# Last samples, squares, decay products and mixer sums of a hybrid decoder trunk put at other steps and on other engines

## The chip, the cores and the metric

One core of one Trainium2 chip. The metric is the device time of one execution in microseconds (us); lower is better. A core has a matrix engine (TensorE, PE in the profile, with PEld for its weight loads), VectorE (DVE), ScalarE (ACT), GpSimd (POOL) and SyncE (SP, which here only issues transfers). Each engine works through its own list of instructions in order; POOL and SP also issue DMAs from their lists. Everything is float32; a product is made as three products of rounded parts ("hi" and "lo").

## The reference

One layer of a decoder trunk, for a prompt of 512 positions and for 8 samples of one new position each, together 520 columns (T) in the kernel. Cut to what the change touches:

```
def mixer(xn, conv_prev, gla_prev, w_in, conv_w, gate_w2, gate_b, gla_norm_g, w_out, chunk):
    proj = xn @ w_in
    bg, cg, hin, q, k, v, og, glr = jnp.split(proj, [...], axis=-1)
    cu, conv_new = causal_dwconv(cg * hin, conv_prev, conv_w)      # width 3
    ya = bg * cu
    logf = jax.nn.log_sigmoid((glr @ gate_w2 + gate_b).astype(f32)) / GATE_TAU
    o, s_new = gla_chunked(qh, kh, vh, lf, gla_prev.astype(f32), chunk)
    var = jnp.mean(o * o, axis=-1, keepdims=True)
    o = o * lax.rsqrt(var + EPS) * gla_norm_g...
    yb = o * silu(og)
    out = jnp.concatenate([ya, yb], axis=-1) @ w_out
```

`gla_chunked` is a gated linear attention of 4 heads (keys of 128, values of 256): within a chunk scores with decays, between chunks a state S of 128 x 256 that decays and grows by keys times values, `S = exp(bC) * S + kdec^T v`, with `kdec = k * exp(bC - b)` and queries `q * exp(b)`. After the mixer come an output projection, a gated convolutional feed-forward and a last norm.

## The kernel before, in words

**Order of the work.** The program is one long list written by hand; `InOrder` (L58) ties the engines to the order in which the program issues. In the first stage the input projection goes in *groups*: `group` (L217) makes one 128-column group of outputs, 16 steps of k with six matmuls each (`span`, `mm3`, L140). Weights come in halves of 8 k: loaded by SP (`fetch`, L101), rounded by ScalarE (`high`, L194), the rest taken by VectorE (`low`, L201).

Beside the matmuls other work is fed in at fixed places of a group. After k = 2, 5, 8, 11, 14 (`BEATS`) `beat` (L157) takes one item from `soon`, then one step of the generator at the head of `queue`, then one item from `side`. At the end of a group, and with `group(True)` also after k = 7, `further` (L213) takes one step of the generator in `extra`.

**Heads.** For each head h the groups are k, q, and two of values; for h = 0 only the values, as k and q come before. Then `gla_head(h, ...)` (L938) goes into `queue` and runs, a step per beat, beside the groups of the next head; the last head (h = 3) runs beside the short convolution's groups (`conv_tile`, L870), three for each of two tiles. A head's steps:

- Gate, cumulative sums, then seven levels of scores, `for i, s in enumerate(LEVELS)` (L1094). For a level POOL makes differences (`ptt`, L290), ScalarE the exponential `e` (L988), VectorE two products `L` (L995), PE the scores (L1055, L1070), VectorE puts them through a mask into `at` (L1077).
- Between them the samples, two at a time: `sample_load` (L1017) has SP load the state and v rows broadcast over the partitions; `sample_pair` (L1026) multiplies v by k on ScalarE (L1029), updates the state on VectorE (L1032) and has SP store it; `sample_out` (L1041) multiplies by the queries on PE (L1043). Samples 0, 2, 4 belong to i = 2, 3, 5, samples 6 to the step of the key transposes.
- At i = 4 to 6 the decays `qb` (for queries) and `kc` (for keys) are made: exponentials on ScalarE (L1109, L1115), differences and both products on POOL (L1118, L1120).
- Key step: PE transposes `kc` (L1126), ScalarE copies it to `kt`.
- Four sub-blocks `for c in range(4)` (L1134): PE makes the output from `at` and v (L1138) and, from c = 1 on, from S and `qb` (L1143); ScalarE copies it into `o` (L1147); PE makes the growth of S (L1152), VectorE copies it (L1154) or updates S with it (L1156).
- Then both squares of `o` on ScalarE (L1181, L1182), their sum on POOL (L1183); a beat later PE sums over partitions (L635, in `rsqrt_sums`); ScalarE takes logarithm and exponential (L1189, L1190); a beat later four Newton steps on VectorE (L293 to L296); a beat later VectorE scales `o` (L1195) and it is stored to `o_d`.

**The mixer's sums.** `mixer_sums` (L779) makes sums and differences of quarters of x for a later product with fewer multiplications (a Strassen-like scheme of seven products). It is the generator in `extra` from head 1 on; for each of four g: a load of four tiles by SP; scaling of two tiles on ScalarE (L794); of two more; two sums on VectorE (L704, L698); stores on POOL, two more sums; then stores with the next load. At the very end three `split`s (L121: ScalarE rounds at L123, VectorE takes the rest at L124) in a single step, while POOL stores the last sum.

**The short convolution.** `conv_tile` computes z, and its convolution `conv` is one item of `side`: the last tap on VectorE (`conv_tap`, L608), then the others (`conv_rest`, L615 and, for samples, L618).

**The next stage** (L1790 on) takes over the memory of the heads' pool; its first weight loads (`second_half`, L833) stand on SP behind that. It loads mixer sums (L1753), splits them and runs the seven products (`up_product`, L1397; weights' parts at L1373 and L1377).

Of the kernel before, what the change touches and what calls it, by code (L numbers as in the profile page):

```python
# [12 lines left out]
AF = mybir.ActivationFunctionType  # L13
# [24 lines left out]
def trunk_kernel(  # L38
# [53 lines left out]
    def tmp():  # L92
        return tp.tile([P, T], F32, tag="t", name="t")
# [195 lines left out]
    def ptt(out, a, b, op):  # L289
        nc.gpsimd.tensor_tensor(out, a, b, op=op)  # L290
# [307 lines left out]
    def bank():  # L598
        return msp.tile([P, 512], F32, tag="ms", name="ms")
# [5 lines left out]
    def conv_tap(c, z, w, taps, j, bias=None):  # L605
        tap = w[:, 2 * taps + j : 2 * taps + j + 1]
        if bias is None:
            nc.vector.tensor_scalar(c[:, :T], z[:, 2:], tap, None, op0=ALU.mult)  # L608
        else:
            nc.scalar.activation(c[:, :T], z[:, 2:], AF.Identity, scale=tap, bias=bias)  # L610
# [8 lines left out]
                c[:, NP:T], st[:, i::2], tap(i), c[:, NP:T], op0=ALU.mult, op1=ALU.add  # L619
            )  # L620

    def conv(z, w, taps, j, st):


        c = tmp()
        conv_tap(c, z, w, taps, j)
        conv_rest(c, z, w, taps, j, st)
        return c

    def rsqrt_sums(src):  # L630

        pss = []
# [67 lines left out]
    def add(out, x, y):  # L700
        nc.vector.tensor_tensor(out, x, y, op=ALU.add)  # L701
# [77 lines left out]
    def mixer_sums():  # L779

        def place(n):
            return yt1.tile([P, T + 3], F32, tag=f"y{n}", name="yx")[:, :T]

        for g in (1, 2, 3, 0):
            xg = [place(n) for n in ("l0 h8 l8 h0" if g % 2 else "l1 l4 h4 h0").split()]
            for q, x in enumerate(xg):
                nc.sync.dma_start(two(x), rows_of(xT_d, "mix", g, q))
            yield  # L790
            for q, x in enumerate(xg):
                m = first_tile("mix", g, q // 2)
                for j, h in enumerate(halves(x)):
                    nc.scalar.activation(h, h, AF.Copy, scale=gmix[:, m + j : m + j + 1])  # L794
                if q == 1:
                    yield
            yield
            t1, t3, t4, b22 = xg
            t2 = place("h1")
            sub(t1, t1, t3)  # L800
            minus(t2, t1, b22)
            yield
            if g:
                for f, t in ((5, t1), (4, t2)):
                    nc.gpsimd.dma_start(mt_d[f - 4, g], t)
            sub(t3, b22, t3)
            minus(t4, t2, t4)
            yield
            nc.gpsimd.dma_start(mt_d[3, g], t4)
            if g:  # L810
                nc.gpsimd.dma_start(mt_d[2, g], t3)
        for f, t in ((5, t1), (6, t3), (4, t2)):
            split(t, *form(f, 0))

# [29 lines left out]
    with ExitStack() as mix:  # L846
# [23 lines left out]
        def conv_tile(j):  # L870
            ps = group()
            cgr = tmp()
            evac(ps, cgr[:, :T])
            ps = group()
            hr = tmp()
            evac(ps, hr[:, :T])
            z = next_z()
            nc.vector.tensor_tensor(z[:, 2:], cgr[:, :T], hr[:, :T], op=ALU.mult)
            keep_last(z, j, 8, new_conv_p, new_conv_s)
            c = []  # L880
            side.append(lambda: c.append(conv(z, cw, 8, j, stc[:, j, :])))
            ps = group()
            bgr, ya = tmp(), tmp()[:, :T]
            if j % 2 == 0:
                even[j] = ya = z[:, 2:]
            evac(ps, bgr[:, :T])
            nc.vector.tensor_tensor(ya, bgr[:, :T], c[0][:, :T], op=ALU.mult)
            mixed_done(j, ya)

        in_order = InOrder(nc.gpsimd.engine, nc.sync.engine).after_all()  # L890
        with ExitStack() as gl:
# [46 lines left out]
            def gla_head(h, q, k, vt):  # L938
# [155 lines left out]
                for i, s in enumerate(LEVELS):  # L1094
                    level_scores(Ls.popleft(), s)
                    if i + 2 < len(LEVELS):
                        products()
                    if i + 3 < len(LEVELS):
                        level(LEVELS[i + 3])
                    if i == 5:  # L1100
                        pos = bank()
                        sample_out(0)
                    if i in (2, 3, 5):
                        s0.append(sample_pair({2: 0, 3: 2, 5: 4}[i], *loaded.popleft()))
                    if i in (0, 2, 5):
                        loaded.append(sample_load({0: 2, 2: 4, 5: 6}[i]))
                    if i == 4:
                        qb = gp.tile([P, 4, P], F32, tag="qb", name="qb")
                        nc.scalar.activation(qb, bc, AF.Exp, scale=1.0 / TAU)  # L1109
                        kc = gp.tile([P, 4, P], F32, tag="e", name="kc", bufs=2)  # L1110
                        ptt(
                            kc, bc[:, :, P - 1 : P].to_broadcast([P, 4, P]), bc, ALU.subtract
                        )
                    if i == 5:
                        nc.scalar.activation(kc, kc, AF.Exp, scale=1.0 / TAU)  # L1115
                        ec = gp.tile([P, 4], F32, tag="ec", name="ec")
                        nc.gpsimd.tensor_copy(ec, qb[:, :, P - 1])
                        ptt(qb, qb, q4, ALU.mult)  # L1118
                    if i == 6:
                        ptt(kc, kc, k4, ALU.mult)  # L1120
                    yield

                o = gp.tile([P, 2, T], F32, tag="o", name="o")
# [2 lines left out]
                    nc.tensor.transpose(pb[:, c * P : (c + 1) * P], kc[:, c, :], idn)  # L1126
                kt = gp.tile([P, 4, P], F32, tag="L", name="kt", bufs=2)
                nc.scalar.activation(kt, pb.rearrange("p (c k) -> p c k", c=4), AF.Copy)
                s0.append(sample_pair(6, *loaded.popleft()))
                yield  # L1130


                S = gp.tile([P, DV], F32, tag="S", name="S")
                for c in range(4):  # L1134
                    po = bank()
                    for d in range(2):
                        out = po[:, d * P : (d + 1) * P]
                        nc.tensor.matmul(  # L1138
                            out, vt[:, c, d * P : (d + 1) * P], at[:, c, :],
                            start=True, stop=c == 0,  # L1140
                        )
                        if c:
                            nc.tensor.matmul(  # L1143
                                out, S[:, d * P : (d + 1) * P], qb[:, c, :],
                                start=False, stop=True,
                            )
                    nc.scalar.activation(  # L1147
                        o[:, :, c * P : (c + 1) * P],
                        po[:, :DV].rearrange("p (d i) -> p d i", d=2), AF.Copy,
                    )  # L1150
                    pS = bank()
                    nc.tensor.matmul(pS[:, :DV], kt[:, c, :], vt[:, c, :], start=True, stop=True)  # L1152
                    if c == 0:
                        nc.vector.tensor_copy(S, pS[:, :DV])  # L1154
                    else:
                        nc.vector.scalar_tensor_tensor(  # L1156
                            S, S, ec[:, c : c + 1], pS[:, :DV], op0=ALU.mult, op1=ALU.add
                        )
                    if c == 1:
                        sample_out(4)  # L1160
                        os_ = gp.tile([P, DV], F32, tag="os", name="os")
                        nc.scalar.activation(os_, pos[:, :DV], AF.Copy)
                    if c == 2:
                        pb = bank()
                        for d in range(2):
                            nc.tensor.matmul(
                                pb[:, d * NS : (d + 1) * NS], os_[:, d * P : (d + 1) * P], sel,
                                start=True, stop=True,
                            )
                        nc.scalar.activation(  # L1170
                            o[:, :, NP:T], pb[:, : 2 * NS].rearrange("p (d b) -> p d b", d=2),
                            AF.Copy,
                        )
                    yield
# [2 lines left out]
                store.dma_start(new_gla_p[0, 0, h], S)  # L1177


                sq, sq2, ro = (tmp()[:, :T] for _ in range(3))  # L1180
                nc.scalar.activation(sq, o[:, 0, :], AF.Square)  # L1181
                nc.scalar.activation(sq2, o[:, 1, :], AF.Square)  # L1182
                ptt(sq, sq, sq2, ALU.add)  # L1183
                yield
                for ps, v in zip(rsqrt_sums(sq), halves(sq2)):
                    nc.scalar.activation(
# [50 lines left out]
            for h in range(NH):  # L1237
# [19 lines left out]
                vt = gp.tile([P, 4, DV], F32, tag="vt", name="vt", bufs=2)  # L1257
                v = []
                for d in range(2):
                    ps = group()  # L1260
                    t = gp.tile([P, T], F32, tag="v", name="v", bufs=2)
                    evac(ps, t)
                    v.append(t)
                    soon.append(lambda: None)
                    soon.append(lambda t=t, vt=vt, d=d: v_rows(t, vt, d, 0, 4))
# [842 lines left out]
```

## Time and profile before

| what | value |
|---|---|
| median of 3 runs | 2139.94 us (2136.82 to 2142.19) |
| profiled execution | 2138.38 us |
| its span, first to last instruction | 2136.7 us |
| mean granted TensorE clock | 0.997 |
| instructions | 44234 |
| HBM read, written | 299.65 MB, 80.31 MB |

The profile is of one execution. A row of a timeline gives start and length in us, the engine, the line of the kernel, the operation and the tiles written and read; in square brackets stands how long the engine was idle before it and what ended that. A row of waits names the waiting engine and line, what it waited for, and total, number and longest. The ends of matmuls are modelled. The same source line can serve many callers, so a row is told apart by its tiles and its time.

### The profile page before, as it was taken

The page shows a single profiled execution, that of the slowest core. Times are in us where ns is not written, and L with a number is a line of the kernel's source. Part 1 is how long each engine was busy: PE and PEld are TensorE (multiplying, and loading weights), DVE is VectorE, ACT ScalarE, POOL GpSimd, SP SyncE. Part 2 cuts the span into 40 slices and gives each one's busy share as a digit, 9 for nine tenths or more (in the row PEclk, how much of TensorE's full clock was granted, in tenths as well). Part 3 has the DMA queues.
Part 4 walks back from the last instruction along what each step waited for, and adds up shares of the span by engine and source line. Part 5 has one row for each costly group of instructions (what it writes and reads, how often), then busy time and mean ns, then how long its engine had stood idle before and what let it go on. Part 6 is the DMA issues. An engine that isn't in the chain of part 4 may idle for free.

```text
span 2136.7 us, 44234 instructions
## 1 busy us (share of the span) xinstructions
PE 2109.9 (99%) x17880; PEld 2088.1 (98%) x17880; DVE 1763.6 (83%) x2349; ACT 1121.8 (53%) x1688; POOL 436.0 (20%) x623
## 2 busy tenths in 40 slices
PE   9999999999999999999999999999999999999997
PEld 8999989999999989999999999999999999999997
DVE  6556675988878898988988988988989778888886
ACT  7444543545544686555555555555555554444445
POOL 4212331112234211211311221212212200300000
PEclk9999999999999999999999999999999999999999
DMA  8455646877798996776776676776766875994734
GB/s 257 131 151 171 180 127 183 222 189 205 187 286 240 268 293 157 183 186 175 181 187 172 182 187 169 181 189 167 189 182 183 292 224 150 274 293 131 222 110 159
DMA packets 467757, 417.30 MB, mean 195 GB/s; under 512 B 21769, under 2 KB 426521, under 8 KB 467409
## 3 DMA queue, kind: packets, MB, share of 16 engines
q1 hardware_dynamic: 424209, 289.84, 47.8%
q0 software_dynamic: 43296, 124.57, 22.3%
q8 instruction: 140, 2.29, 0.5%
q14 instruction: 64, 0.52, 0.1%
q10 hardware_dynamic: 48, 0.07, 0.0%
HBM read 299.65 MB, written 80.31 MB: 178 GB/s over the span
## 4 chain that ended last, share of the span: by engine, by line
PE 62%; DMA 1%; DVE 1%; issue 1%; ACT 0%; POOL 0%; ACTq 0%; DVEq 0%; SPq 0%; POOLq 0%
PE mm L1397 29%; PE ms L1397 12%; PE x L1640 7%; PE y L1640 7%; PE f L1640 3%; PE e L1640 3%; PE mm L140 2%; DMA ssq<-fh 1%; DMA x_d<-acc 0%; PE ms L1998 0%; DMA yl<-t_d 0%; DVE yl L124 0%; DVE lo L1377 0%; DVE s L1318 0%; ACT y L2061 0%
## 5 line engine op out<-in xcount | busy, mean ns | idle before, releaser
L1397 PE MATMUL mm<-yl,hi 128*128 128x260 f32 x1792 | 504.1, 281 | 2.8 <-DVE yl L124 2.8
L1397 PE MATMUL mm<-yh,hi 128*128 128x260 f32 x1792 | 502.5, 280 | 0.6 <-DVE t L701 0.6
L1397 PE MATMUL mm<-yh,lo 128*128 128x260 f32 x1792 | 502.0, 280 | 0.8 <-DVE lo L1377 0.8
L1373 ACT ACTIVATE hi<-raw 128x1024 fp32r<-128x1024 f32 x336 | 354.4, 1055 | 245.4 <-issue 89.3
L1377 DVE TENSOR_TENSOR lo<-raw,hi 128x1024 fp32r<-128x1024 f32 x336 | 410.2, 1221 | 44.6 <-ACT hi L1373 40.8
L1377 DVE TENSOR_TENSOR lo<-s,hi 128x1024 fp32r<-128x1024 f32 x252 | 309.4, 1228 | 131.3 <-ACT hi L1373 129.9
L1373 ACT ACTIVATE hi<-s 128x1024 fp32r<-128x1024 f32 x252 | 266.3, 1057 | 233.2 <-PE ms L1397 97.3
L1397 PEld LDWEIGHTS mm<-yl,hi 128*128 128x128 f32 x1792 | 336.6, 188 | 3.7 <-DVE yl L124 3.7
L1397 PEld LDWEIGHTS mm<-yh,lo 128*128 128x128 f32 x1792 | 337.8, 189 | 1.2 <-DVE lo L1377 1.2
L1397 PEld LDWEIGHTS mm<-yh,hi 128*128 128x128 f32 x1792 | 337.7, 188 | 0.8 <-issue 0.8
L1397 PE MATMUL ms<-b,hi 128*128 128x260 f32 x1408 | 264.9, 280 | 0.0
L1397 PEld LDWEIGHTS ms<-b,hi 128*128 128x128 f32 x1408 | 222.0, 188 | 0.0
L1640 PE MATMUL y<-form,hi 128*128 128x260 f32 x1120 | 211.6, 281 | 0.6 <-DVE acc L1659 0.6
L1640 PE MATMUL x<-form,hi 128*128 128x260 f32 x1120 | 211.7, 281 | 0.1
L1318 DVE TENSOR_TENSOR s<-s,raw 128x1024 f32<-128x1024 f32 x168 | 205.2, 1222 | 2.9
L1397 PE MATMUL ms<-b,lo 128*128 128x260 f32 x704 | 197.0, 280 | 0.0
L1640 PEld LDWEIGHTS y<-form,hi 128*128 128x128 f32 x1120 | 176.5, 188 | 0.9 <-ACT hi L1373 0.7
L1640 PEld LDWEIGHTS x<-form,hi 128*128 128x128 f32 x1120 | 176.5, 188 | 0.6 <-issue 0.4
L1640 PE MATMUL x<-form,lo 128*128 128x260 f32 x560 | 157.0, 280 | 0.1
L1640 PE MATMUL y<-form,lo 128*128 128x260 f32 x560 | 156.9, 280 | 0.1
L1397 PEld LDWEIGHTS ms<-b,lo 128*128 128x128 f32 x704 | 132.0, 187 | 0.0
L1397 PE MATMUL mm<-bh,hi 128*128 128x260 f32 x448 | 125.5, 280 | 1.0 <-DVE acc L1659 1.0
(402 smaller groups left out, 4847.3 us busy)
## 6 DMA issues: line engine op xcount, KB each, us to landing
raw<-in_w_up_dram SPq DMA_DIRECT2D x176, 512.0 KB, 4.7
raw<-in_w_down_dram SPq DMA_DIRECT2D x96, 512.0 KB, 7.3
raw<-in_w_in_dram SPq DMA_DIRECT2D x92, 512.0 KB, 5.0
form<-f_d SPq DMA_DIRECT2D x126, 260.0 KB, 6.0
raw<-raw POOLq DMA_DIRECT2D x59, 512.0 KB, 5.3
f_d<-t POOLq DMA_DIRECT2D x80, 260.0 KB, 5.5
raw<-in_w_out_dram SPq DMA_DIRECT2D x32, 512.0 KB, 10.8
form<-g_d POOLq DMA_DIRECT2D x42, 260.0 KB, 7.5
```

What stands on the lines that cost most here:

```text
L140: nc.tensor.matmul(o, w, xx, start=first and i == 0, stop=last and i == 2)
L1318: return lambda: nc.vector.tensor_tensor(out, x, y, op=ALU.add)
L1373: nc.scalar.activation(his[i], src, AF.Copy)
L1377: nc.vector.tensor_tensor(los[i], src, his[i].bitcast(F32), op=ALU.subtract)
L1397: nc.tensor.matmul(st["bank"][b], w[:, k, :], x, start=b not in st["used"] and k == 0 and j == 0, stop=k == 7 and j == 2, skip_group_check ...
L1640: nc.tensor.matmul(ps[:, m, :], w[:, k, m * P : (m + 1) * P], x, start=b not in st["used"] and k == 0 and j == 0, stop=k == 3 and j == 2, ...
```

## The change

The computation stays as it is; steps change their place in the lists and three kinds change their engine.

- The last pair of samples goes from the key step to the end of sub-block c = 0; what reads it, `sample_out(4)` with the copy, from c = 1 to c = 2; the sums over samples from c = 2 to c = 3.
- The product for `qb` goes from POOL at i = 5 to VectorE at the key step; that for `kc` from POOL to VectorE at i = 6.
- The squares of the first 384 columns of `o` are made at the start of c = 3, those of the remaining 136 columns where all were made before; their sum goes from POOL to VectorE.
- The last tap of the short convolution goes from VectorE to ScalarE as a `side` item of its own; `conv_rest` follows as the next item, a beat later. `conv` is gone.
- `mixer_sums` yields after each of its three last splits, and the first value group of heads 1 to 3 calls `further` at k = 7 as well.

```diff
@@ mixer_sums
         for f, t in ((5, t1), (6, t3), (4, t2)):
             split(t, *form(f, 0))
+            yield
@@ conv_tile
-            c = []
-            side.append(lambda: c.append(conv(z, cw, 8, j, stc[:, j, :])))
+            c = tmp()
+            tap = cw[:, 16 + j : 17 + j]
+            side.append(lambda: nc.scalar.activation(c[:, :T], z[:, 2:], AF.Copy, scale=tap))
+            side.append(lambda: conv_rest(c, z, cw, 8, j, stc[:, j, :]))
...
-            nc.vector.tensor_tensor(ya, bgr[:, :T], c[0][:, :T], op=ALU.mult)
+            nc.vector.tensor_tensor(ya, bgr[:, :T], c[:, :T], op=ALU.mult)
@@ gla_head
                         nc.gpsimd.tensor_copy(ec, qb[:, :, P - 1])
-                        ptt(qb, qb, q4, ALU.mult)
                     if i == 6:
-                        ptt(kc, kc, k4, ALU.mult)
+                        nc.vector.tensor_tensor(kc, kc, k4, op=ALU.mult)
                     yield
...
                 nc.scalar.activation(kt, pb.rearrange("p (c k) -> p c k", c=4), AF.Copy)
-                s0.append(sample_pair(6, *loaded.popleft()))
+                nc.vector.tensor_tensor(qb, qb, q4, op=ALU.mult)
                 yield
...
+                def squares(u):
+                    nc.scalar.activation(sq[:, u], o[:, 0, u], AF.Square)
+                    nc.scalar.activation(sq2[:, u], o[:, 1, u], AF.Square)
+
                 for c in range(4):
+                    if c == 3:
+                        sq, sq2, ro = (tmp()[:, :T] for _ in range(3))
+                        squares(slice(0, 3 * P))
                     po = bank()
...
-                    if c == 1:
+                    if c == 0:
+                        s0.append(sample_pair(6, *loaded.popleft()))
+                    if c == 2:
                         sample_out(4)
                         os_ = gp.tile([P, DV], F32, tag="os", name="os")
                         nc.scalar.activation(os_, pos[:, :DV], AF.Copy)
-                    if c == 2:
+                    if c == 3:
                         pb = bank()
...
-                sq, sq2, ro = (tmp()[:, :T] for _ in range(3))
-                nc.scalar.activation(sq, o[:, 0, :], AF.Square)
-                nc.scalar.activation(sq2, o[:, 1, :], AF.Square)
-                ptt(sq, sq, sq2, ALU.add)
+                squares(slice(3 * P, T))
+                add(sq, sq, sq2)
                 yield
@@ groups of the heads
                 for d in range(2):
-                    ps = group()
+                    ps = group(h > 0 and d == 0)
```

More of the change, by code (lines that the diff above doesn't have):

```diff
@@ L620, in conv_rest @@
             )
[L622 to L628, printed above, removed]
     def rsqrt_sums(src):
```

## The prediction, on record before the changed kernel ran

> **What bounds the kernel now.** I read the page's first part, then the list of who waited for whom on PE, the busy times in stretches around each wait, the timelines of the other engines there, and SP's waits where the next stage begins.
>
> ```profile
> PE 2109.9 (99%) x17880; PEld 2088.1 (98%) x17880; DVE 1763.6 (83%) x2349; ACT 1121.8 (53%) x1688; POOL 436.0 (20%) x623
> ```
>
> PE is busy 2109.9 of 2136.7 us, so no edit on another engine can win more than the time PE stands still or runs slowly. The edits touch the heads of the GLA mixer (about 60 to 350 us). PE's waits there, first those from 80 to 130 us (the first head), then those from 260 to 345 (the end of the third and the last):
>
> ```profile
> PE ms L1143 <- DVE S L1154: 2.1, 1, 2.1
> PE ms L1070 <- DVE L L995: 0.2, 1, 0.2
> ```
>
> ```profile
> PE ms L1070 <- DVE L L995: 2.9, 3, 1.6
> PE ms L635 <- POOL t L290: 0.8, 1, 0.8
> PE ms L1043 <- DVE s L1032: 0.3, 1, 0.3
> ```
>
> Those are 2.1 + 0.2 + 2.9 + 0.8 + 0.3 = 6.3 us in seven waits (columns: total, times, longest). The one of 2.1 us has a tail:
>
> ```profile
> 121.80:125.20 3.40, 1.32 (x11) 1.13 (x10) 3.27 (x6) 1.68 (x4) 0.00 (x0) 1.00 0.27 83
> 125.20:128.60 3.40, 3.40 (x18) 1.94 (x17) 2.77 (x5) 0.77 (x2) 0.00 (x0) 0.50 0.57 153
> ```
>
> The first columns are the stretch and PE's busy time; the third from the end is the granted clock. After 3.4 us in which PE was busy for 1.32, it ran 3.4 us at 0.50: half of 3.4, or 1.7 us, lost.
>
> A wait also hides a part of itself:
>
> ```profile
> 806.40 5.71 PE mm L1397 x48
> L1397 PE MATMUL mm<-yh,lo 128*128 128x260 f32 x1792 | 502.0, 280 | 0.8 <-DVE lo L1377 0.8
> ```
>
> Undisturbed matmuls follow each other every 5.71 / 48 = 119 ns but are drawn 280 ns long, so a gap shows up to 0.16 us too short: at most 1.1 us over seven waits; I take 0.5. At stake in the heads: 6.3 + 0.5 + 1.7 = 8.5 us.
>
> **Part by part: what goes.** *First head, 2.1 us and the slow clock.*
>
> ```profile
> 121.36 0.91 ACT L1029 ACTIVATE vb<-vb,k 128x256 f32<-128x256 f32 x2 [4.49 <-DMA vb<-v_d]
> 121.90 0.88 DVE L1032 SCALAR_TENSOR_TENSOR s<-s,asm,vb 128x256 f32<-128x256 f32 x2 [5.32 <-ACT vb L1029]
> 123.95 0.42 DVE L1154 COPY S<-ms 128x256 f32<-128x256 f32 x1
> ```
>
> VectorE sits 5.32 us in front of the last samples, whose v rows are still on the way, and the copy of S that PE needs is queued behind. The change asks for those samples after that copy, so the copy goes at once. What stands behind the samples then is the update of S one sub-block later; the samples end at 121.90 + 0.88 = 122.8, in time for it, and the samples' own reader moves a sub-block later too. The wait goes, and with it the idle stretch ahead of the slow clock: 2.1 + 1.7.
>
> The Trainium skill (TensorE: Matmul & The Clock Gate, "HAM oscillation — how this bites in real kernels") puts the limit at PE-idle gaps over about 3.4 us; by it a gap of 2.1 us halves nothing, and the 1.7 would not belong to this wait. The trace disagrees: clock 0.50 directly after a gap of 2.1. I go by the row and keep the rule as a rival.
>
> *Last head, 2.9 and 0.3 us.*
>
> ```profile
> 309.66 0.64 ACT L123 ACTIVATE yh<-yx 128x520 fp32r<-128x520 f32 x1 [1.10 <-DMA mt_d<-yx]
> 311.15 0.61 ACT L988 ACTIVATE e<-e 128x512 f32<-128x512 f32 x1
> 317.70 1.45 POOL L290 TENSOR_TENSOR kc<-kc,k 128x512 f32<-128x512 f32 x1
> 317.95 1.49 DVE L995 TENSOR_TENSOR L<-e,k 128x256 f32<-128x256 f32 x1
> 112.21 0.41 DVE L995 TENSOR_TENSOR L<-e,k 128x256 f32<-128x256 f32 x1
> ```
>
> The mixer's sums end in three splits issued in one go, the third waiting for a store; the exponential (L988) that VectorE's product (L995) needs is behind them. With an extra call in each head's first value group the sums run three calls ahead, so the splits come one per group and end a group earlier. Of POOL's products the row shows a second harm: beside one, L995 takes 1.49 us instead of 0.41. Both go to VectorE, so the 1.08 goes too. The convolution's first tap leaves VectorE and its rest comes a beat later, behind the products. I let the 2.9 and the 0.3 that follows from them go; the first head's 0.2 goes with POOL's product there (below).
>
> *Third head, 0.8 us.*
>
> ```profile
> 271.23 0.62 ACT L1181 ACTIVATE t<-o 128x520 f32<-128x520 f32 x1
> 272.45 1.29 POOL L290 TENSOR_TENSOR t<-t 128x520 f32<-128x520 f32 x1 [25.21 <-ACT t L1182]
> 273.79 1.14 PE L635 MATMUL ms<-t,ones 128*128 128x260 f32 x4 [0.78 <-POOL t L290]
> L293 DVE TENSOR_TENSOR t<-t 128x520 f32<-128x520 f32 x4 | 2.8, 701 | 9.7 <-ACT t L1190 9.6
> ```
>
> PE was ready at 273.79 - 0.78 - 0.16 = 272.85. Of the squares 136 of 520 columns are left at this step (two instructions, each between 0.16 us, by columns, and the 0.62 of all 520; I take the middle, 0.39), the sum takes 0.70 on VectorE: 271.23 + 0.78 + 0.70 = 272.7. It goes, with little to spare.
>
> **What comes.** *The decayed keys on VectorE, first head: +1.5 us.* PE transposes them at L1126. The extra call also puts two of the mixer's sums ahead of them on VectorE, in the middle of this value group:
>
> ```profile
> 107.48 1.62 POOL L290 TENSOR_TENSOR qb<-qb,q 128x512 f32<-128x512 f32 x1
> 107.28 0.69 DVE L704 TENSOR_TENSOR yx<-yx 128x520 f32<-128x520 f32 x1
> 108.00 1.67 DVE L698 SCALAR_TENSOR_TENSOR yx<-yx 128x520 f32<-128x520 f32 x1
> 109.70 0.77 DVE L1249 SCALAR_TENSOR_TENSOR q<-mm,R 128x260 f32<-128x260 f32 x2
> 110.38 0.61 DVE L1077 COPY_PREDICATED at<-mask,ms 64x128 f32<-64x128 uint8 x2
> 111.02 1.27 DVE L995 TENSOR_TENSOR L<-e,q 128x256 f32<-128x256 f32 x1
> 112.55 1.21 DVE L201 TENSOR_TENSOR lo<-raw,hi 128x1024 fp32r<-128x1024 f32 x1
> 113.79 0.92 DVE L1077 COPY_PREDICATED at<-mask,ms 64x128 f32<-64x128 uint8 x2
> 114.75 0.88 DVE L1032 SCALAR_TENSOR_TENSOR s<-s,asm,vb 128x256 f32<-128x256 f32 x2
> 115.66 0.92 DVE L1077 COPY_PREDICATED at<-mask,ms 64x128 f32<-64x128 uint8 x2
> 115.63 0.60 PE L1126 MATMUL ms<-idn,kc 128*128 128x128 f32 x4
> ```
>
> VectorE has no gap here and ends at 115.66 + 0.92 = 116.6. Without POOL's products L698 falls from 1.67 to 0.70 (L704 of the same size takes 0.69) and L995 from 1.27 to 0.41: 1.8 earlier, 114.8. Added: two sums, 1.4, and the product, 0.70 (L293's 701 ns, for 520 columns): 116.9. PE asks at 115.63, or 115.4 without the 0.2 that it waited just before. So a new wait of 1.5. Bounds: 0, if POOL's conflicts cost VectorE more than I took off, and 2.1, if nothing comes off the last two of them.
>
> *The last convolution's rest, +1.6 us at the start of the next stage.* Where the last head ends, its rest moves from in front of the four Newton steps to behind them, that is ahead of the scaling of o at L1195:
>
> ```profile
> 343.28 0.75 DVE L615 SCALAR_TENSOR_TENSOR t<-zpad,par,t 128x512 f32<-128x512 f32 x1
> 344.09 0.75 DVE L615 SCALAR_TENSOR_TENSOR t<-zpad,par,t 128x512 f32<-128x512 f32 x1
> 348.90 1.43 DVE L1195 SCALAR_TENSOR_TENSOR o<-o,par,t 128x520 f32<-128x520 f32 x2
> SPq L833 <- DMA o_d<-o: 6.7, 1, 6.7
> 371.55 1.06 ACT L1373 ACTIVATE hi<-raw 128x1024 fp32r<-128x1024 f32 x1 [5.13 <-DMA raw<-in_w_in_dram]
> 375.00:400.00 25.00, 23.44 (x190) 22.64 (x189) 24.88 (x36) 14.94 (x26) 2.01 (x3) 1.00 0.80 226
> ```
>
> The rest is two such instructions, each with a small one for the samples behind it: 344.09 - 343.28 = 0.81 from start to start, 1.6 us for both. The newton steps wait for ACT, so nothing makes up for it. SP stands 6.7 us for the store of o to land before it loads the next stage's weights; ACT then waits for such a load until 371.55, and VectorE is busy 24.88 of 25 us from 375 to 400, while PE loses 25 - 23.44 = 1.56 us. A chain that full has nothing to absorb a late start: +1.6. Bounds: 0 and 1.6, and 1.7 more if the longer gap halves the clock.
>
> *At nothing:* the q product (0.70) and the later samples fill VectorE's 5.32 us of idleness, and cost their length if that is gone. The tap on ACT lies beside the head's last steps. Loads of x now come half a group ahead of their first use at two places (48 x 119 ns = 5.7 us); a late one holds ACT's next weight half, which has about half a group in hand. Bounds there: 0 to 1.7 each.
>
> Sum: 8.5 - 1.5 - 1.6 = 5.4 us. The profiled execution took 2138.38 us (span 2136.7 and 1.7 around it), so 2133.0 in its own time; it lies 1.6 under the median, 2139.94, from which the same step gives 2134.5 us.
>
> **Rivals.**
> *Both costs hidden (0.27).* VectorE gets to the keys in time, and the store's delay is lost among other transfers: all 8.5, 2131.4. For: engines off the path have slack in the later heads. Against: no gap in either VectorE stretch.
> *The slow clock does not go (0.15).* Clock and gap are not tied, or the longer gap at 382 us starts another 3.4 us at half speed: 5.4 - 1.7 = 3.7, 2136.2. By the skill's rule the first of these holds.
> *Waits only change place (0.09).* The S updates wait behind the late samples one sub-block on, and the last head finds its next late operand: 0, 2139.9. Against: the samples had landed by then.
> *VectorE becomes the bound (0.07), slower.* Each of the four heads waits for its keys at L1126. It decides from a gap of some 2.1 us, where the clock halves as well: 4 x (2.1 + 1.7) = 15.2, with 1.6 at the next stage, less 8.5: +8.3, 2148.2. For: the first head has 1.5 already. Against: the later heads show VectorE idle before L1032 and L1077.
>
> **How the numbers follow.** The forecast has 0.42. About 0.3%, or 6.4 us, is what a measurement of this kernel tells from no change; 5.4 lies inside it. Faster: the first rival and a quarter of the forecast's spread, 0.38. Same: the rest of the forecast, the clock, the changed places: 0.55. Slower: 0.07. The range goes from the first rival with 1.4 for run-to-run spread, 2130, to no gain with 1, 2141.
>
> **What would show it.** Right: no wait at L1143 for S, none at L635 for POOL, the clock at 1.00 from 125 to 129 us; a wait at L1126 on VectorE's kc of about 1.5 us near 116; o's store landing 1.6 us later behind PE's L635, and PE's waits between 380 and 400 us grown by as much. Wrong: a wait at L1126 in every head, or L1070 waits still there in the last head, or PE's loss after 380 us unchanged.

## The result, and the profile after

| | before | after |
|---|---|---|
| median of 15 runs each, same chips | 2138.95 us (2135.74 to 2142.19) | 2134.65 us (2131.71 to 2137.37) |
| ratio, 95% interval | | 0.998 (0.9972 to 0.9988) |
| profiled execution | 2138.38 us | 2136.04 us |
| its span | 2136.7 us | 2134.3 us |

4.3 us less: a gain of 0.2%, whose interval leaves out 1 and which lies under the 0.3% that a few runs can tell. The profiled execution of one experiment (e12) was disturbed and isn't read.

After's page, first part, and its waits of PE from 55 to 345 us (the heads):

```profile
PE 2109.1 (99%) x17880; PEld 2087.9 (98%) x17880; DVE 1765.6 (83%) x2359; ACT 1124.0 (53%) x1698; POOL 419.2 (20%) x611
```

```profile
PE ms L1120 <- DVE kc L1114: 1.7, 2, 1.4
PE ms L1038 <- DVE s L1027: 0.2, 1, 0.2
```

Of seven waits of 6.3 us one of 0.2 is left, and the keys' transposes (L1126 before, L1120 now) have two new ones, 1.4 in the first head and 0.3 in the last. The first head, by stretches (PE's busy time second, the granted clock third from the end):

```profile
121.80:125.20 3.40, 3.40 (x30) 3.37 (x29) 1.93 (x5) 2.12 (x4) 0.00 (x0) 1.00 0.79 223
125.20:128.60 3.40, 3.40 (x30) 3.35 (x30) 1.61 (x2) 0.39 (x1) 0.00 (x0) 1.00 1.01 301
```

PE is busy throughout and at full clock where it was busy for 1.32 of 3.40 us and then ran at 0.50. VectorE and ACT there, and PE's transposes:

```profile
111.64 0.43 DVE L990 TENSOR_TENSOR L<-e,q 128x256 f32<-128x256 f32 x1
115.32 0.69 DVE L696 TENSOR_TENSOR yx<-yx 128x520 f32<-128x520 f32 x1
115.94 0.69 DVE L690 SCALAR_TENSOR_TENSOR yx<-yx 128x520 f32<-128x520 f32 x1
...
117.59 0.69 DVE L1114 TENSOR_TENSOR kc<-kc,k 128x512 f32<-128x512 f32 x1
118.20 0.68 DVE L1123 TENSOR_TENSOR qb<-qb,q 128x512 f32<-128x512 f32 x1
121.98 0.90 ACT L1024 ACTIVATE vb<-vb,k 128x256 f32<-128x256 f32 x2
122.14 0.43 DVE L1156 COPY S<-ms 128x256 f32<-128x256 f32 x1 [2.12 <-PE ms L1154]
118.43 0.63 PE L1120 MATMUL ms<-idn,kc 128*128 128x128 f32 x4 [1.36 <-DVE kc L1114]
```

The two sums of the extra call (L696, L690) stand ahead of the keys' product, which ends at 118.28, and PE waits 1.36 for it. The copy of S waits only for PE now. Where the next stage begins, first two rows of before's timeline, then of after's (the PE rows are the first matmul of the group after the convolutions):

```profile
346.24 0.70 DVE L293 TENSOR_TENSOR t<-t 128x520 f32<-128x520 f32 x1
...
353.44 0.28 PE L140 MATMUL mm<-bh,hi 128*128 128x260 f32 x1
```

```profile
341.57 0.70 DVE L293 TENSOR_TENSOR t<-t 128x520 f32<-128x520 f32 x1 [2.40 <-ACT t L1192]
345.72 1.43 DVE L1197 SCALAR_TENSOR_TENSOR o<-o,par,t 128x520 f32<-128x520 f32 x2
348.78 0.28 PE L140 MATMUL mm<-bh,hi 128*128 128x260 f32 x1
367.88 1.06 ACT L1375 ACTIVATE hi<-raw 128x1024 fp32r<-128x1024 f32 x1 [4.78 <-DMA raw<-in_w_in_dram]
```

Then after's waits of SP (335 to 400) and of PE (360 to 402), and the stretch from 375:

```profile
SPq L826 <- DMA o_d<-o: 10.7, 1, 10.7
...
PE mm L1399 <- DVE lo L1379: 1.4, 2, 1.0
PE mm L1399 <- DVE t L693: 0.6, 1, 0.6
```

```profile
375.00:400.00 25.00, 22.72 (x182) 21.72 (x181) 24.85 (x36) 14.92 (x25) 3.48 (x5) 1.00 0.80 207
```

PE loses 25 - 22.72 = 2.28 us there, where it was 1.56; its waits of 360 to 402 us were 1.4 us in all before and are 2.0. From the Newton steps to the scaling it was 348.90 - 346.24 = 2.66 us (the scaling at 348.90 stands in the prediction) and is 345.72 - 341.57 = 4.15: the convolution's rest stands between. Against that group the scaling goes from 348.90 - 353.44 = -4.54 to -3.06, 1.5 later, and ACT's first weights from 371.55 - 353.44 = 18.11 to 19.10, 1.0 later.

**Where the 4.3 us come from.** I subtract the start of the same matmul in the two traces. The heads' first group starts at 51.20 before and at 52.77 after: the stage ahead, whose code is the same, took 1.6 longer in this execution (over thirteen profiles it starts between 51.18 and 52.80). The heads take 353.44 - 51.20 = 302.24 and 348.78 - 52.77 = 296.01, so -6.2. The next stage's first 588 matmuls take 73.10 and 74.07, so +1.0. Together -5.2. Further on one thing more differs:

```profile
789.40:792.80 3.40, 1.54 (x11) 1.14 (x10) 3.22 (x5) 2.35 (x5) 0.86 (x1) 1.00 1.10 338
792.80:796.40 3.60, 3.01 (x14) 3.01 (x15) 3.60 (x5) 2.44 (x5) 0.00 (x0) 0.53 1.18 273
```

In code that the change doesn't touch, from 489 to 844 us, this execution lost 1.6 us against the profile of before. PE waits there in both: it is idle for 5.1 of the 30 us from 775 to 805 before, and for 5.3 after. Only the stretch at half clock is new, and e1 and e11 (below) lose 1.7 and 1.6 in the same code at full clock. So the span falls by 2.4 only: the comparison of one execution with another hides half of the gain that the stages show.

### The profile page after: what moved, and what is told of

Its sections match the earlier page's. It is cut to its first block, busy times and chain, and to the rows that moved or that the text cites. A ratio compares the mean times of both kernels' runs of the same rounds, so it can differ in the third digit from the quotient of the medians.

```text
span 2134.3 us, 44244 instructions
## 1 busy us (share of the span) xinstructions
PE 2109.1 (99%) x17880; PEld 2087.9 (98%) x17880; DVE 1765.6 (83%) x2359; ACT 1124.0 (53%) x1698; POOL 419.2 (20%) x611
## 4 chain that ended last, share of the span: by engine, by line
PE 62%; DMA 2%; issue 1%; DVE 0%; ACT 0%; POOL 0%; ACTq 0%; DVEq 0%; POOLq 0%
PE mm L1399 29%; PE ms L1399 12%; PE x L1642 7%; PE y L1642 7%; PE f L1642 3%; PE e L1642 3%; PE mm L140 2%; DMA x_d<-acc 1%; DMA ssq<-fh 1%; PE ms L2000 0%; DVE lo L1379 0%; ACT y L2063 0%; PE ms L1770 0%; DVE yl L124 0%; DVE b L124 0%
```

## The experiments

Edits are against the changed kernel, except for e8. Times are medians; ratios are to before on the same chip, with 95% intervals (the changed kernel: 0.998, 0.9972 to 0.9988).

**e1: the keys' wait.** Head 1 makes no extra call, so the two sums leave the first head's key step.

```diff
-                    ps = group(h > 0 and d == 0)
+                    ps = group(h > 1 and d == 0)
```

> The changed kernel without the extra call of the mixer's sums in the first head's value group (head 1 keeps its old calls, heads 2 and 3 the new ones). Theory (order on VectorE): the 1.4 us wait of PE for the decayed keys near 117 us is the two sums ahead of the product; it falls to 0 to 0.2, time 2134.65 - 1.4 = 2133.2. Rival (VectorE's total is the bound): the sums come later and the same 1.4 us shows at another wait before 145 us; time 2134.7. A cost of up to 0.7 in the last head is possible with both, as the last split now falls between its levels.

2133.85 us, ratio 0.9974 (0.9963 to 0.9984). PE's waits in the heads:

```profile
PE ms L1065 <- DVE L L990: 0.5, 1, 0.5
PE ms L1120 <- DVE kc L1114: 0.5, 2, 0.3
...
```

The wait of 1.4 is gone (0.2 is left in that head), so it was those two sums. 0.5 comes back in the last head, where the mixer's sums now end one call later; the heads take 6.8 us less than before, not 6.2. Against the changed kernel the median moves by 0.8, inside the intervals.

**e2: the late store.** The first tap of the second convolution tile is issued at once, so its rest moves up a beat, in front of the Newton steps.

```diff
-            side.append(lambda: nc.scalar.activation(c[:, :T], z[:, 2:], AF.Copy, scale=tap))
+            first_tap = lambda: nc.scalar.activation(c[:, :T], z[:, 2:], AF.Copy, scale=tap)
+            first_tap() if j == 1 else side.append(first_tap)
```

> The changed kernel with the second tile's first tap issued at once on ScalarE, so that the rest of that convolution again stands ahead of the last head's Newton steps. Theory: the store of o is issued 1.7 us earlier behind the last head's partition sum (8.8 us after the group's start instead of 10.6), the first weights of the next stage come 1.0 us earlier, and PE's waits between 370 and 400 us fall by 1.0; time 2133.7. Rival (the burst of transfers after 350 us sets it, not the store): store earlier, waits after 370 us unchanged; time 2134.7.

2134.2 us, 0.9973 (0.9963 to 0.9982). The store was issued 1.2 us earlier against the group behind the convolutions (-2.96, was -1.77), and still PE waited more after 360:

```profile
PE mm L1400 <- DVE lo L1380: 1.4, 2, 1.0
PE mm L1400 <- ACT ms L1410: 0.9, 1, 0.9
PE mm L1400 <- DVE t L693: 0.6, 1, 0.6
```

In this execution the rival was right: ACT's first weights came at 19.88, no earlier. The same edit inside e7 and e10 gave 18.39 and 18.86. So one profile can't settle it; the whole row of them says more (below).

**e3: the samples back.** The last samples and their readers return to their places of before, the samples behind the q product; all else stays changed.

```diff
                 nc.vector.tensor_tensor(qb, qb, q4, op=ALU.mult)
+                s0.append(sample_pair(6, *loaded.popleft()))
...
-                    if c == 0:
-                        s0.append(sample_pair(6, *loaded.popleft()))
-                    if c == 2:
+                    if c == 1:
                         sample_out(4)
...
-                    if c == 3:
+                    if c == 2:
```

> The changed kernel with the last samples back in the key step (behind the q product), and their readers at their old places. Theory, row of before taken over: PE waits 2.1 us for S near 125 us again, with or without 3.4 us at half clock: 2136.8 to 2138.5. Rival (the gains do not add up): the wait for the keys now holds PE up by 1.4 us just before, and the samples are asked for earlier, so that S is in time: wait under 0.3, 2134.7.

2135.37 us, 0.9979 (0.9971 to 0.9988). No wait for S returns, the clock stays at 1.00 in the heads, and these take the same 6.2 us less. Why, in four rows:

```profile
118.20 0.63 PE L1120 MATMUL ms<-idn,kc 128*128 128x128 f32 x4 [1.36 <-DVE kc L1114]
120.33 0.91 ACT L1024 ACTIVATE vb<-vb,k 128x256 f32<-128x256 f32 x2 [0.88 <-DMA vb<-v_d]
122.93 0.42 DVE L1157 COPY S<-ms 128x256 f32<-128x256 f32 x1
124.77 0.39 PE L1146 MATMUL ms<-qb,S 128*128 128x128 f32 x2
```

Before, the v rows were in 121.36 - 115.63 = 5.7 us after the transposes; here it is 120.33 - 118.20 = 2.1. The copy of S is done at 123.35, 1.4 us ahead of PE. So the gains don't add: with the other edits in, the samples may stand where they stood.

**e4: the mixer's sums back.** No extra call, the three splits in one step.

```diff
             split(t, *form(f, 0))
-            yield
...
-                    ps = group(h > 0 and d == 0)
+                    ps = group()
```

> The changed kernel with the mixer's sums at their old calls and the three splits in one step again. Theory (splits ahead of the exponential held the last head up): L1070's waits come back there, 1.7 to 3.2 us, and the keys' wait of 1.4 in the first head goes; time 2134.65 + 0.3 to 1.8 = 2135.0 to 2136.5. Rival (POOL's products beside VectorE held it up): the last head stays without waits, only the 1.4 goes: 2133.2.

2136.34 us, 0.9989 (0.998 to 0.9997).

```profile
PE ms L1064 <- DVE L L989: 2.3, 1, 2.3
...
PE ms L1119 <- DVE kc L1113: 0.2, 1, 0.2
```

```profile
308.20:311.60 3.40, 1.11 (x22) 0.73 (x22) 3.30 (x8) 3.10 (x7) 1.11 (x2) 1.00 0.06 17
311.60:315.00 3.40, 3.14 (x14) 2.21 (x12) 3.25 (x7) 0.63 (x1) 0.37 (x2) 0.50 0.40 104
```

The keys' 1.4 goes and the last head's wait is back as one of 2.3, with half clock behind it. Between the same matmuls the first head takes 1.2 less than in the changed kernel and the last one 3.3 more, and the heads together 1.9 more. So the calls bring more in the last head than they cost in the first, as the theory had it; the half clock cost about 0.8 there (an estimate: 3.3 less the wait of 2.3 and the 0.16 that a wait hides), not 1.7.

**e5: the squares back** at their old place in one go, the sum on POOL (`ptt`).

```diff
-                    if c == 3:
-                        sq, sq2, ro = (tmp()[:, :T] for _ in range(3))
-                        squares(slice(0, 3 * P))
...
-                squares(slice(3 * P, T))
-                add(sq, sq, sq2)
+                sq, sq2, ro = (tmp()[:, :T] for _ in range(3))
+                squares(slice(0, T))
+                ptt(sq, sq, sq2, ALU.add)
```

> The changed kernel with all squares and their sum at the old place, the sum on POOL. Theory: PE's partition sum waits 0.8 us for POOL again in the third head, nowhere else: 2135.5. Rival (the wait came from ScalarE's and VectorE's lag, which the other edits removed): no wait, 2134.7.

2136.41 us, 0.9988 (0.9979 to 0.9997). Exactly the old wait is back:

```profile
...
PE ms L627 <- POOL t L290: 0.8, 1, 0.8
...
```

The median lost 1.8, more than 0.8, but the intervals overlap; the profile also has a half-clock stretch at 381 us. By the stages the heads take 1.0 more than in the changed kernel, the wait and what it hides, and the next stage 1.2 more, behind weights that came late (below).

**e6: both decay products back on POOL.**

```diff
+                        ptt(qb, qb, q4, ALU.mult)
                     if i == 6:
-                        nc.vector.tensor_tensor(kc, kc, k4, op=ALU.mult)
+                        ptt(kc, kc, k4, ALU.mult)
...
-                nc.vector.tensor_tensor(qb, qb, q4, op=ALU.mult)
```

> The changed kernel with both decay products back on POOL at i = 5 and 6. Theory: PE's waits for the keys (1.4 in the first head, 0.3 in the last) go, as POOL makes them beside VectorE; VectorE's two-input operations beside POOL are stretched again (L698's pair from 1.4 to 2.4, L995 from 0.41 to 1.3 and more), which shows as 0 to 1 us of waits for L: 2133.0 to 2134.0. Rival (POOL's products were the larger part of the gain): waits for L of 2 us and more come back, 2135 to 2137.

2134.39 us, 0.9978 (0.9969 to 0.9987).

```profile
PE ms L1065 <- DVE L L990: 1.1, 1, 1.1
PE ms L917 <- DVE v L603: 0.4, 1, 0.4
...
```

```profile
108.39 1.67 DVE L690 SCALAR_TENSOR_TENSOR yx<-yx 128x520 f32<-128x520 f32 x1
111.41 1.18 DVE L990 TENSOR_TENSOR L<-e,q 128x256 f32<-128x256 f32 x1
```

Beside POOL's products the same two operations as before stretch (1.67 and 1.18, against 0.70 and 0.43 in the changed kernel). This agrees with what the Trainium skill says of a port pair that the two engines share (SBUF — State Buffer, "Who interferes with whom"): a VectorE instruction with two inputs in SBUF contends there with a GpSimd instruction that reads SBUF. Waits of 1.1 in the last head and 0.4 in the third come, the keys' 1.7 goes, and the heads take 6.4 less than before, where the changed kernel's take 6.2 less. Net nothing: moving the two products together brought no time by itself (e10 prices them one by one).

**e7: e1 and e2 together.** The edits of both.

> The changed kernel with both repairs: no extra call of the sums in the first head's value group, and the second tile's first tap at once on ScalarE. Theory: both costs go, 1.4 + 1.0: 2132.2, 0.3% under the kernel before. Rival (gains do not add up, what is won ahead is lost in the next stage's start): PE's waits between 370 and 400 us grow by what was won, 2133.7 or above.

2134.21 us, 0.9978 (0.9969 to 0.9987). In the profile both parts are there (the heads take 6.9 less than before, the next stage 0.3 more instead of 1.0), and half clock at 792 us and the waits around it take 1.9 back. The median shows no sum of gains: 2 us above what was expected, and open by how much that is chance.

**e8: the samples alone,** in the kernel before.

```diff
-                s0.append(sample_pair(6, *loaded.popleft()))
...
-                    if c == 1:
+                    if c == 0:
+                        s0.append(sample_pair(6, *loaded.popleft()))
+                    if c == 2:
                         sample_out(4)
...
-                    if c == 2:
+                    if c == 3:
```

> The kernel before with only the last samples and their readers moved. Theory: the 2.1 us wait for S near 122 us goes and with it the half clock after it: 2138.95 - 2.1 - 1.7 = 2135.1. Rival one (half clock not tied to that gap): clock 0.50 somewhere near 125 us still, 2136.8. Rival two (wait only changes its place): as much wait at the next sub-block, 2138.9.

2135.98 us, 0.9987 (0.9978 to 0.9996).

```profile
PE ms L1070 <- DVE L L995: 2.4, 3, 2.0
...
```

```profile
121.80:125.20 3.40, 3.40 (x29) 3.35 (x29) 2.51 (x6) 2.12 (x4) 0.00 (x0) 1.00 0.47 149
...
309.10:312.40 3.30, 1.22 (x22) 0.73 (x22) 3.24 (x8) 2.92 (x7) 1.36 (x2) 1.00 0.03 10
312.40:315.90 3.50, 3.38 (x13) 2.57 (x14) 3.41 (x6) 0.45 (x1) 3.42 (x3) 0.51 0.49 125
```

The first head gains 3.9 us: 2.1 and 1.7 as forecast. The last head's wait, 1.6 at its longest in the profile of before, is 2.0 here, and now this one is followed by half clock. So over all heads 3.2 of the 3.9 are left, and 2.8 in the medians.

**e9 and e12: the store later.** One empty beat, and then two, in the last head in front of the scaling.

```diff
                 newton(ro, sq2, sq, nc.vector)
                 yield
+                if h == NH - 1:
+                    yield
```

> The changed kernel with one empty beat more ahead of the last head's scaling, so that o is stored some 2.9 us later. Theory (the store gates the next stage's weights): ScalarE gets the first of them 2.9 us later than in the changed kernel, measured from the end of the last convolution group (19.1 becomes 22.0), and PE loses 2.9 us more between 365 and 400 us, with a half clock perhaps: 2137.5 to 2139. Rival (the burst of transfers sets it): the weights come at 19 to 20 as in the runs so far, time 2134.7 to 2135.5.

2134.04 us, 0.9982 (0.9973 to 0.9991). The store did not move (-1.76): VectorE comes to the scaling without waiting for PE at a beat. So the run tests nothing and is a repeat of the changed kernel: its heads take 296.01 us, as there, and its next stage 74.27, where it was 74.07.

> The changed kernel with two empty beats more in the last head alone, between its Newton steps and the scaling of o. One empty beat (the run before of this kind) left the store where it was, because VectorE waits for nothing there; with two, the scaling stands behind the weights' lower half of k = 11, which VectorE makes from weights that come with the group. Theory (o's store holds SP's first load of the next stage, and what comes later is lost one to one): the store's issue moves from -1.8 to about -0.4 us against the start of the group behind the convolutions, ScalarE's first weights of the next stage from 19.1 (19.1 to 19.9 in five executions with the same store) to 20.3 or later, and PE's time of the stage's first 588 matmuls from 74.1 to 75.3 or more; the median goes from 2134.65 to about 2135.9. Rival (the weights' arrival is set by the queue of transfers there and its scatter of about 1 us, not by the store): the store moves, but first weights within 19.1 to 19.9, the 588 matmuls within 74.1 to 74.9, the median at 2134.6 within 0.5.

2134.81 us, 0.9985 (0.9976 to 0.9994). The ratio leans to the theory by 0.0005, or 1.1 us, and its interval holds both answers. As its profiled execution was disturbed, no row shows whether the store moved: not settled by this.

**e10: the best of the parts.** The keys' product back on POOL, the q product left on VectorE, and the edit of e2.

```diff
-                        nc.vector.tensor_tensor(kc, kc, k4, op=ALU.mult)
+                        ptt(kc, kc, k4, ALU.mult)
```

> The changed kernel with the key product alone back on POOL (the q product stays on VectorE), and the second tile's first tap at once on ScalarE. Theory: PE's waits for the keys (1.7 us in two) go and nothing comes for them, as VectorE loses one short product and meets POOL once; the store of o is 1.2 us earlier: 2134.65 - 1.9 - 0.7 = 2132.0. Rival (VectorE beside POOL): a wait for L of 1 us as with both products back, 2133.5 to 2134.5.

**2131.23 us**, 0.9967 (0.9955 to 0.9979), the lowest of all. Its waits in the heads, and the keys:

```profile
PE ms L1066 <- DVE L L991: 0.8, 1, 0.8
...
```

```profile
110.08 1.52 POOL L290 TENSOR_TENSOR kc<-kc,k 128x512 f32<-128x512 f32 x1 [0.56 <-ACT kc L1111]
115.32 0.60 PE L1121 MATMUL ms<-idn,kc 128*128 128x128 f32 x4
```

POOL has the keys ready at 111.60, 3.7 us before PE takes them. The heads take 7.5 us less than before, with one wait for L of 0.8, which the theory did not have. e2's edit changes the heads by 0.02 us, so they price the products: the keys' on POOL brings 1.3 (e10 against e2), and q on VectorE 1.2 (e10 against e6). Against the changed kernel the medians differ by 3.4 us; the two intervals still share 0.9972 to 0.9979, and e10 has six runs. The heads and the next stage account for 1.3 + 0.2 of the 3.4; where the rest comes from wasn't found.

**e11: the convolution as before,** tap and rest on VectorE in one item.

```diff
-            side.append(lambda: nc.scalar.activation(c[:, :T], z[:, 2:], AF.Copy, scale=tap))
-            side.append(lambda: conv_rest(c, z, cw, 8, j, stc[:, j, :]))
+            def conv():
+                conv_tap(c, z, cw, 8, j)
+                conv_rest(c, z, cw, 8, j, stc[:, j, :])
+            side.append(conv)
```

> The changed kernel with the convolution as it was: the last tap on VectorE, tap and rest as one item. Theory: o is stored 1.7 us earlier, the next stage's first weights come 1.0 us earlier and PE loses 1.0 us less after 365 us, while in the last head the wait for L behind the convolution (0.2 to 0.3 us) is back: 2133.9. Rival (the order of the convolution is worth more in the last head than it costs): 2 us and more of waits for L in the last head, 2135.5 or above.

2134.37 us, 0.9977 (0.9968 to 0.9986).

```profile
PE ms L1123 <- DVE kc L1117: 1.6, 2, 1.4
PE ms L1068 <- DVE L L993: 1.0, 1, 1.0
```

The next stage gets 0.8 back (73.30 us for its 588 matmuls). In the last head PE waits 1.0 for L (L1068), where 0.2 to 0.3 was expected; but coming later, it gets 0.8 of that back at the samples' product (L1038 in the changed kernel, whose wait for s is gone). Between the same matmuls the heads take only 0.2 us longer (296.17 against 296.01). So the tap's move serves the last head by 0.2 us and costs 0.8 behind it.

**The store, over all profiles.** Store's issue and ACT's first weights, each against the start of the group behind the convolutions, and PE's time for the stage's 588 matmuls (4 short ones among them, L1905 in before, not counted); worked out from start times in each trace:

| kernel | store | first weights | 588 matmuls |
|---|---|---|---|
| before, e8, e11 | -3.5 to -3.2 | 18.1 to 18.4 | 73.1 to 73.4 |
| e7, e10, e2 | -3.0 | 18.4, 18.9, 19.9 | 73.4, 73.9, 74.9 |
| e5 | -2.0 | 20.3 | 75.3 |
| after, e1, e3, e4, e6, e9 | -1.8 | 19.1 to 19.9 | 74.1 to 74.9 |

PE's time follows the first weights one to one: it ends 55.0 us behind them in every profile, also in e5, whose half clock at 381 us added nothing there. The weights follow the store loosely: a mean of 18.7 for the six early stores and of 19.6 for the seven late ones, but each group spreads over more than a microsecond, and e2 is an early store with late weights. What makes that scatter wasn't found.

## Why the prediction was right, point by point

- **The time.** 2134.5 forecast, 2134.65 measured. That they agree so closely is partly luck: the forecast started from 2139.94, the median of three runs, where fifteen give 2138.95, and the medians fell by 4.3 (2.6 to 6.0 by the interval), not by 5.4. By the same steps in the traces: heads -7.0 forecast (8.5 less the keys' 1.5), -6.2 measured; next stage +1.6, measured +1.0; sum -5.4, measured -5.2. Why the medians fell by 0.9 less than these stages stays open.
- **First head, 2.1 and the half clock: right.** e8 does this part alone and gains 3.9. But e3 shows that the step isn't needed where the others are made. I argued from one waiting row and did not ask when the load would be requested in the new order. SP requests the last v rows behind the store of earlier samples, which VectorE makes: 65.4 us after the heads' start before, 65.3 in e6 with POOL's products, 63.6 in e3, where VectorE works without them.
- **The tie of gap and clock: right here, its price by luck.** After gaps of 2.1 (before), 2.0 (e8) and 2.3 us (e4) the clock halved, and where the gap goes it stays at 1.00. The limit of the Trainium skill (TensorE: Matmul & The Clock Gate, "HAM oscillation — how this bites in real kernels"), gaps over about 3.4 us, does not agree with these rows. But the length of a gap doesn't decide alone: each of the three lay whole in one step of a grid of 3.41 us (last section), and this grid stands elsewhere in each execution. So the 1.7 was counted in full from one execution, where others with the same gap need not pay it.
- **Last head, 2.9 and 0.3: right, with two readings mended.** e4 gives 2.3 back without the calls. I gave POOL's product 1.08 of it; e6, with POOL's products and the calls, has 1.1 there. And the tap on ACT, which I gave no value of its own there, takes away a wait of 1.0 by e11, but only 0.2 of time. 0.2 of the 0.3 stayed.
- **Third head, 0.8: right.** e5 has it back to the tenth.
- **Keys, +1.5: right,** 1.4 in the first head and 0.3 in the last. e1 shows that the two sums cause it.
- **Next stage, +1.6: the direction right, the size too large.** The scaling came 1.5 later, as forecast; the weights 1.0 later. "A chain that full has nothing to absorb a late start" was the step that failed: the transfers between store and weights scatter by more than what was left to explain. As e2's weights came late behind an early store, and e12 doesn't settle it, how much of the 1.0 is the store's stays open.
- **The 0.5 hidden in short gaps: borne out.** The keys' waits drawn as 1.36 and 0.29 us in after cost PE 1.52 and 0.45 against e6, where they are gone: 0.16 hidden in each. The three waits now left hide as much again: 8.5 - 1.7 - 0.2 - 0.5 = 6.1; 6.2 was measured.
- **Not foreseen:** half-clock stretches elsewhere (793 us in after, 381 in e5, 792 in e7) that decide what one profile says. An execution's mean clock was 0.995 to 0.997 in 15 of 33 executions of before on one chip, and 0.998 or 0.999 in all 15 of the changed kernel. A stretch of 3.4 us at half clock moves it by 1.7 / 2135 = 0.0008, so before seems to have more of them. But the mean doesn't tell them one by one: each profile also ends with 6.3 to 9.0 us at half clock, which moves it by 0.0015 to 0.0021, and of the six profiles with one stretch inside, two read 0.997 (before, e4) and four 0.998 (after, e5, e7, e8). How many such stretches before has at the median, where I had counted one as if it came each time, stays open.
- **The rivals.** "Both costs hidden" fell: both are in the trace. "Waits only change place" holds in small: e1, e11 and e6 each remove a cost and get waits of 0.5, 1.0 and 1.5 elsewhere. VectorE did not become the bound: later heads wait 0.3 at most for their keys.

## What to carry to other kernels

Where one engine is 99% busy, list its waits with what is queued behind each and price each edit by them; then undo the edits one by one, since several may remove the same wait (e3), others only trade it (e6), and a wait that shows may cost less than it is long (e11). Move an operation off a shared-memory neighbour only as far as it pays: the q product on VectorE with the keys' product left on POOL gave the shortest heads and the lowest median (e10), though its interval still meets the changed kernel's. And judge a gain of 0.2% by many runs and by differences within a stage, not by two spans.

## What the runs showed of the hardware that was not expected

- The traces' clock record shows a grid of 3.41 us. Six profiles have one half-clock stretch inside the run (before, after, e4, e5, e7, e8). Each lasts one step of 3.41 us and lies a whole number of steps ahead of the slow clock at that execution's end: (2128.84 - 125.21) / 587 = 3.4133 before, (2127.61 - 793.00) / 391 = 3.4133 after. In the step ahead of the six PE was busy for 1.03 to 1.36 us. In the other steps that the half clock did not follow, 8045 in 13 profiles, it was busy for 1.96 us or more. So what counted here is how much idle time fell into one step, not the length of a wait. Three steps, of before, e8 and after:

```profile
312.92:316.33 3.41, 2.04 (x26) 1.14 (x27) 3.38 (x6) 2.54 (x5) 2.23 (x3) 1.00 0.02 5
309.03:312.45 3.42, 1.24 (x23) 0.73 (x22) 3.36 (x8) 3.04 (x7) 1.41 (x2) 1.00 0.04 13
789.58:793.00 3.42, 1.36 (x10) 0.95 (x8) 3.39 (x5) 2.37 (x4) 0.86 (x1) 1.00 1.10 338
```

Before's wait of 1.6 us in the last head (312.41 to 314.02) was cut by the step's edge at 312.92, and the clock stayed at 1.00. e8's of 2.0 (309.05 to 311.04) lay whole in one step, and the clock halved, as it did behind the third. Over the 13 profiles the first edge came 0.1 to 2.9 us after the heads' first matmul, so which waits halve the clock changes from execution to execution.

- The same transfers behind a store issued at the same -2.96 landed 1.5 us apart in two kernels that differ in one call of the mixer's sums, in the first head's value group (first weights at 18.4 and 19.9 us in e7 and e2).
- An empty beat does not delay an engine that waits for nothing there (e9): the store stayed at -1.76 us.
